# A mixed convolution, pooling and MLP layer on one core: weight splits, a broadcast row and side work given other places in the order

## The chip, the cores and the metric

The kernel runs on one core of one Trainium2 chip. The metric is the device time of one execution in microseconds (us), the median of several runs. In the profile PE is the matrix engine (TensorE), PEld its weight loads, DVE the vector engine, ACT the scalar engine, POOL GpSimd and SP the engine that issues most DMAs. L145 is line 145 of the kernel.

## What is computed

One decoder layer on x of 2048 tokens by 1024 channels, all in float32. Shift, scale and gate of both halves come from a vector c through one large matrix.

```
mod = silu(c) @ w_ada + b_ada                      # sh1, sc1, g1, sh2, sc2, g2
h = x * (1 + sc1) + sh1
z = h @ w_in                                       # 1024 -> 3 * 512 + 512
y_conv = gate_b * short_conv(gate_c * v_conv)      # 3 taps, causal
y_pool = (means over 2, 4, 8, 16 tokens minus token) @ w_pool * pool_scale
x = layer_norm(alpha * x + (1 + g1) * (concat(y_conv, y_pool) @ w_out))
h = x * (1 + sc2) + sh2
f = square(relu(h @ w_mlp_in)) @ w_mlp_out         # 1024 -> 4096 -> 1024
x = layer_norm(alpha * x + (1 + g2) * f)
```

## The kernel before

**Splits and triples.** A float32 matrix is used as the sum of two parts, hi and lo. `split` (L144 to L146) casts the source to hi on ACT (L145) and subtracts hi from the source on DVE (L146). `mm3` (L151) multiplies with three matmuls (L152 to L154): hi by hi, hi by lo, lo by hi. One call of `mm3` is called a triple here; it counts a beat while side work is open.

**Block schemes.** Large products are not done as eight block products but by schemes with fewer products of sums of blocks (seven for two by two blocks; 26 in the last stage). So there is much vector work on sums of blocks: of weights before a product, of results behind it.

**Stages.** The tokens are in two blocks of 1024. For each block: `in_proj_0` or `in_proj_1` (the input projection, four groups; in the second block `in_proj_1`, seven products of eight triples for each group), `out_proj` (seven products, 112 triples) and `first_map` (the MLP's first matrix, "MLP-up": eight groups `up` of seven products of eight triples). `first_map` ends in sums of result blocks (`sums`, L1107), stored to DRAM in `usum` by POOL (`stored`, L1105). Some sums are written in place over cells that have been stored before, so DVE waits there until the store has read them. At the end of block 0 the sums of the last group are kept as `owed` and are done within `in_proj_1` (`flush`). After both blocks `down` does the second matrix in 26 products (`PRODUCTS`) of four steps (gp) each, with operands loaded from `usum` and from the MLP's second weights, raw (`in_w`) or summed (`wsum`).

**The product of seven.** `seven` (L626) makes `product(i, ...)`. It takes the next weight block of the generator `ready` (load into an r tile on SP, and for `block_weights`, L591, four sums on DVE when the third block is taken), splits it into two w tiles, and issues the 24 matmuls. The eviction or sum of the result comes behind it in the caller. There are six w tiles (three pairs) and five r tiles; the 28 h tiles hold the other operands.

**Order.** Instructions are written out in program order; the framework lays them out on each engine's queue by the time at which it reckons them ready, the earlier in the program first among those that are ready. Each queue then runs strictly in order. `issue_after` ties an instruction behind another of its engine; `behind(ins)` (L578) makes everything issued inside it wait for `ins`, on whatever engine.

**Side work.** `sums_down` (L1184) makes the summed weights `wsum` by DMAs from DRAM to DRAM on POOL, 80 of 512 KB: a copy, and later one that adds (L1188). One is issued at each triple whose number is in `W_BEATS`, counted from the start of `in_proj_1`; that stage has the triples 1 to 224, `out_proj` 225 to 336, `first_map` of block 1 those from 337 to 784. `first_map` of block 1 has 48 beats of its own for `second_side`: loads and dot products for the gate g2 (`gate_dot`), and `gate_row` with `row_by_dram` (L223): the 1024 gates are transposed, stored to `grow` and read back into all partitions (`bc`). A job is begun at its beat and finished three beats later.

**Down.** `operand(n, gp)` (L1237) loads and splits four steps ahead. `later = prepared(...)` (L1192) prepares the residual: it loads the rows `ag` and `ab` (L287, scaled in L1194 and L1195), then one tile of `nsave` after another, works on it and stores it to `rsave`; two jobs in each product. `finish` (L1287) reads it, for the first time at product 10.

```
            if n > 0 and gp % 2 == 0:
                next(later, None)
```

The functions that the change touches, and what calls them:

Of the kernel before, what the change touches and what calls it, by code (L numbers as in the profile page):

```python
# [13 lines left out]
P = 128  # L14
# [5 lines left out]
KD = D // P  # L20
# [7 lines left out]
WINDOWS = (2, 4, 8, 16)  # L28
HALO = 16
Q = 256  # L30
W_BEATS = {*range(64, 208, 7), *range(360, 776, 7)}
QUARTERS = slice(0, 256), slice(256, 512)

SLOTS = 26
# [68 lines left out]
G2 = 40  # L103
# [4 lines left out]
def tile_hybrid_layer(ctx: ExitStack, tc: tile.TileContext, opening, xT, x, wada, win,  # L108
                      wins, wpool, wout, wmix, w1, w2, rows, out):
    nc = tc.nc  # L110
# [11 lines left out]
    def mk(p, shape, dt, tag, bufs):  # L122
        names[0] += 1
        return p.tile(shape, dt, name=f"{tag}_{names[0]}", tag=tag, bufs=bufs)
# [4 lines left out]
    def t_o(w=T, dt=F32):  # L129
        return mk(big, [P, w], dt, "o", 10)  # L130
# [7 lines left out]
    def t_ps():  # L138
        return mk(pp, [P, H], F32, "ps", 8)

    def t_tmp():
        return mk(sm, [P, H], F32, "tmp", 1)

    def split(src, hi, lo):  # L144
        high = nc.scalar.copy(hi, src)  # L145
        return high.ins, nc.vector.tensor_tensor(lo, src, hi.bitcast(F32), op=ALU.subtract).ins  # L146


    beside_products, beats = [], [0]

    def mm3(ps, whi, wlo, xhi, xlo, first, last, goes_on=False):  # L151
        nc.tensor.matmul(ps, whi, xhi, start=first, stop=False, skip_group_check=goes_on)  # L152
        nc.tensor.matmul(ps, whi, xlo, start=False, stop=False, skip_group_check=goes_on)  # L153
        done = nc.tensor.matmul(ps, wlo, xhi, start=False, stop=last, skip_group_check=goes_on)  # L154
        if beside_products:
            beats[0] += 1
            if beats[0] in W_BEATS:
                with behind(done.ins):
                    next(beside_products[0], None)
# [42 lines left out]
    mod = cp.tile([P, 48], F32, name="mod")  # L202
# [17 lines left out]
            nc.scalar.copy(dst[:, hs], banks[h])  # L220


    def row_by_dram(dst, cols, n):  # L223
        ps, r = t_ps(), t_tmp()
        nc.tensor.transpose(ps[:KD, :P], cols, ident)
        nc.scalar.copy(r[:KD, :P], ps[:KD, :P])
        nc.gpsimd.dma_start(grow[n].rearrange("(k p) -> k p", k=KD), r[:KD, :P])  # L227
        nc.gpsimd.dma_start(dst, grow[n].partition_broadcast(P))

    cond_banks = spread(silu)  # L230
    keep_warm(ident, ident, WARM[1])
# [22 lines left out]
    grow = tc.dram_tile([2, D], F32, name="grow")  # L254
# [17 lines left out]
    def dot(f, r):  # L272
        return nc.vector.scalar_tensor_tensor(r, r, 1.0, cond, op0=ALU.mult, op1=ALU.mult,
                                              accum_out=acc[:, f : f + 1])
# [71 lines left out]
    def parts(src, t=t_h):  # L346
        hi, lo = t(), t()
        split(src, hi, lo)
        return hi, lo
# [227 lines left out]
    @contextmanager  # L577
    def behind(ins):  # L578
        traced = nc.cur_bb.bb.instructions
        n = len(traced)  # L580
        yield
        for i in traced[n:]:
            if i.engine != nc.tensor.engine:
                tc.add_manual_dep(i, ins.name, mybir.DependencyInfo(
                    mybir.DependencyClass.NoSync if i.engine == ins.engine else mybir.DependencyClass.Sync,
                    mybir.DependencyReason.DATA), reason="behind")
# [39 lines left out]
    def seven(ready, B, first_w=None):  # L626
        made = [first_w] if first_w else []

        def product(i, banks, new):
            hi, lo = made.pop() if made else parts(next(ready), t_w)  # L630
            for p in range(2):
                if new:
                    banks[p] = t_ps()
                for k in range(4):
                    bh, bl = B[ORDER[i][1], k // 2]
                    ks = slice((k % 2) * H, (k % 2) * H + H)
                    cs = slice(p * H + k * P, p * H + k * P + P)
                    mm3(banks[p], hi[:, cs], lo[:, cs], bh[:, ks], bl[:, ks], new and k == 0, k == 3,
                        not new)

        return product

# [549 lines left out]
    def prepared(order, raw, g2):  # L1192
        ag, ab = row(t_o(D), rows[0]), row(t_o(D), rows[1])
        nc.scalar.mul(ag, ag, ALPHA)  # L1194
        nc.scalar.mul(ab, ab, ALPHA)  # L1195

        def gated_weights(r):
            for hs in halves:
                tt(r[:, hs], r[:, hs], g2[:, halves[0]], ALU.mult)

        def residual(r):
            tt(r, r, ag, ALU.mult)
            tt(r, r, ab, ALU.add)

        jobs = [(nsave[t], rsave[t], residual) for t in order]
        jobs += [(w2[w, gp], wsum[W_KEPT - 8 + i, gp], gated_weights) for i, w in enumerate(raw) for gp in range(4)]
        loaded, worked = [], []
        for job in jobs + [None, None]:
            if worked:
                nc.sync.dma_start(*worked.pop())  # L1210
            if loaded:
                (_, dst, work), r = loaded.pop()
                work(r)
                worked.append((dst, r))
            if job:
                r = t_r()
                nc.sync.dma_start(r, job[0])
                loaded.append((job, r))
            yield

    def down(g2, close):
# [15 lines left out]
        def operand(n, gp):  # L1237
            s, ws, sign = PRODUCTS[n][:3]
            if n >= last - 1:
                ws = ((W_KEPT + n - last + 1, 1),)  # L1240
            r = t_r()
            nc.sync.dma_start(r, usum[s, gp].rearrange("p b g n -> p (b g n)"))
            qs = [t_w(F32) for _ in ws]
            for q, (w, _) in zip(qs, ws):
                nc.sync.dma_start(q, w2[w, gp] if w < 8 else wsum[w - 8, gp])
            q = qs[0]
            for more, (_, plus) in zip(qs[1:], ws[1:]):
                tt(q, q, more, ALU.add if plus > 0 else ALU.subtract)
            hi, lo = t_h(), t_h()
            if sign > 0:  # L1250
                split(r, hi, lo)
            else:
                nc.scalar.mul(hi, r, -1.0)
                nc.vector.scalar_tensor_tensor(lo, r, -1.0, hi.bitcast(F32), op0=ALU.mult, op1=ALU.subtract)
            return hi, lo, *parts(q)

        def unit(ps, i, ops, first, end, goes_on, cs=slice(0, H)):
            uh, ul, wh, wl = ops
            for p in range(2):
                us = slice((i // 2) * H + p * Q + (i % 2) * P, (i // 2) * H + p * Q + (i % 2) * P + P)  # L1260
                ws_ = slice(p * H + cs.start, p * H + cs.stop)
                mm3(ps, uh[:, us], ul[:, us], wh[:, ws_], wl[:, ws_], first and p == 0, end and p == 1, goes_on)
# [40 lines left out]
        def last_product(ops):  # L1303
            for i, R in enumerate(rows_of(LATE)):
                for cs in [lo_] if i < 3 else QUARTERS:
                    ps = banks[(last - 1) % 2][i][:, cs]
                    for gp in range(4):
# [9 lines left out]
        ready = [operand(*x) for x in stream[:4]]  # L1317
        later = prepared(sorted(range(16), key=lambda R: (min(final[R % 8 // 2, d] for d in range(2)), R)),
                         [PRODUCTS[n][1][0][0] for n in (last - 1, last)], g2)
        for k, (n, gp) in enumerate(stream):  # L1320
            if n == last:
                break
            if k + 4 < len(stream):
                ready.append(operand(*stream[k + 4]))
            ops = ready.pop(0)
            _, _, _, new, reads = PRODUCTS[n]
            if gp == 0 and new:
                banks[n % 2] = [t_ps() for _ in range(4)]
            if n > 0 and gp % 2 == 0:
                next(later, None)  # L1330
            for i in range(4):
                unit(banks[n % 2][i], i, ops, new and gp == 0, gp == 3, not new)
            if gp == 3:
                for t, d, c in reads:
                    read(t, d, c, banks[n % 2])
                    if final[t, d] == n:
                        finish(t, d)
# [88 lines left out]
    def gate_dot(f):  # L1426
        r = t_o(D)
        nc.sync.dma_start(r, wada[f - G1])
        yield
        dot(f, r)  # L1430

    def gate_row():
        biased(G2, G2 + KD)
        g2 = mk(sm, [P, D], F32, "bc", 1)
        yield
        row_by_dram(g2, mod[:, G2 : G2 + KD], 1)
        gate.append(g2)

    def timed(jobs):
        due = {}  # L1440
        for beat in range(48):
            for _ in due.pop(beat, ()):
                pass
            if beat in jobs:
                next(jobs[beat])
                due[beat + 3] = jobs[beat]
            yield
# [3 lines left out]
        return timed(dict(zip((5, 11, 13, 18, 20, 26), sums)))  # L1451

    def second_side():
        rows_ = [gate_dot(f) for f in range(G2, G2 + KD)] + [gate_row()]
        return timed(dict(zip((4, 6, 11, 13, 18, 20, 25, 27, 33), rows_)))

    gate = []

# [25 lines left out]
    ready = []  # L1484
# [64 lines left out]
```

## Time and profile before

| | |
|---|---|
| median of 3 runs | 1732.97 us (1732.69 to 1733.95) |
| profiled execution | 1726.58 us, span 1724.7 us |
| granted clock of TensorE, mean | 0.994 |
| PE busy | 1692.8 us (98%) |
| DVE busy | 1402.6 us (81%) |
| ACT busy | 844.1 us (49%) |
| POOL busy | 377.9 us (22%) |
| moved by DMA | 469.45 MB, 272 GB/s |

Busy time is the share of the span in which an engine works on an instruction; waits are listed by the engine that waited, with the line that released it. The stages in the profile's time: block 0 to about 580 us, `in_proj_1` to 740, `out_proj` of block 1 to about 820, its `first_map` to about 1140, then `down`.

### The profile page before, as it was taken

To read this page: it belongs to the slowest core of one execution; us is meant where nothing else is said; L and a number is where in the kernel's file an instruction comes from. 1 tells how busy PE (TensorE), PEld (TensorE's weight loads), DVE (VectorE), ACT (ScalarE), POOL (GpSimd) and SP (SyncE) were. 2 spreads that over 40 slices of the span, in tenths; PEclk is the share of its full clock that TensorE was granted. 3 is DMA by queue.
4 is the path that set the end of the run, shared out by engine and by line. 5 is a ranking of instruction groups with operands and counts; after the bars stand their busy time and mean duration, and the time that the engine had idled before them with its cause. 6 is when DMAs were issued, how large, how long until landed. Compare 5 with 4: busy or idle time off the path is not lost. (4 is left out here: it accounts for less than half of the span.)

```text
span 1724.7 us, 22033 instructions
## 1 busy us (share of the span) xinstructions
PE 1692.8 (98%) x7519; PEld 1399.9 (81%) x7519; DVE 1402.6 (81%) x2138; ACT 844.1 (49%) x1160; POOL 377.9 (22%) x687
## 2 busy tenths in 40 slices
PE   9999999999999899999999999889999999999998
PEld 8888888888888688888887888768888888888886
DVE  8997798898886766896887777658888777897898
ACT  6323358556555733446754445346543434434554
POOL 0222221344543202201154555430000000000000
PEclk9999999999999999999999999999999999999999
DMA  9998876567764847975899999899999989786782
GB/s 386 349 334 321 305 261 254 194 202 247 235 219 145 269 147 209 262 253 209 259 265 278 274 271 275 239 333 363 346 342 339 351 321 359 273 324 225 259 293 98
DMA packets 149216, 469.45 MB, mean 272 GB/s; under 512 B 20456, under 2 KB 20976, under 8 KB 149104
## 3 DMA queue, kind: packets, MB, share of 16 engines
q1 hardware_dynamic: 93184, 303.38, 48.9%
q0 software_dynamic: 55920, 164.67, 31.2%
q8 instruction: 58, 0.95, 0.2%
q14 instruction: 54, 0.44, 0.1%
HBM read 350.01 MB, written 159.91 MB: 296 GB/s over the span
## 5 line engine op out<-in xcount | busy, mean ns | idle before, releaser
L154 PE MATMUL ps<-h,w 128*128 128x512 f32 x1312 | 512.9, 392 | 13.0 <-DVE w L146 12.9
L152 PE MATMUL ps<-h,w 128*128 128x512 f32 x1312 | 512.4, 391 | 1.0 <-ACT w L145 0.9
L153 PE MATMUL ps<-h,w 128*128 128x512 f32 x1312 | 512.7, 391 | 0.0
L153 PE MATMUL ps<-h,h 128*128 128x512 f32 (+1 forms) x1064 | 413.7, 389 | 8.4 <-DVE h L146 8.4
L152 PE MATMUL ps<-h,h 128*128 128x512 f32 (+1 forms) x1064 | 413.1, 388 | 0.9 <-DVE h L162 0.9
L154 PE MATMUL ps<-h,h 128*128 128x512 f32 (+1 forms) x1064 | 413.4, 389 | 0.0
L154 PEld LDWEIGHTS ps<-h,w 128*128 128x128 f32 x1312 | 247.6, 189 | 66.6 <-DVE w L146 15.6
L152 PEld LDWEIGHTS ps<-h,w 128*128 128x128 f32 x1312 | 247.2, 189 | 54.0 <-ACT w L145 2.3
L153 PEld LDWEIGHTS ps<-h,w 128*128 128x128 f32 x1312 | 247.2, 188 | 51.7
L1105 POOL DMA_DIRECT2D usum<-o x416 | 226.0, 555 | 271.9 <-DVE o L162 147.5
L145 ACT CAST w<-r 128x1024 fp32r<-128x1024 f32 x156 | 164.1, 1053 | 208.1 <-PE ps L153 187.1
L146 DVE TENSOR_TENSOR w<-r,w 128x1024 fp32r<-128x1024 f32 x156 | 189.9, 1220 | 69.2 <-ACT w L145 68.1
L153 PEld LDWEIGHTS ps<-h,h 128*128 128x128 f32 x1064 | 200.3, 188 | 50.1 <-DVE h L146 9.2
L145 ACT CAST h<-r 128x1024 fp32r<-128x1024 f32 (+1 forms) x136 | 136.2, 1008 | 213.5 <-PE ps L153 89.0
L152 PEld LDWEIGHTS ps<-h,h 128*128 128x128 f32 x1064 | 200.2, 188 | 42.0 <-DVE h L162 1.1
L154 PEld LDWEIGHTS ps<-h,h 128*128 128x128 f32 x1064 | 200.3, 188 | 40.6
L162 DVE TENSOR_TENSOR o<-o,o 128x256 f32<-128x256 f32 (+2 forms) x458 | 201.0, 486 | 20.7 <-DMA usum<-o 18.6
L146 DVE TENSOR_TENSOR h<-r,h 128x1024 fp32r<-128x1024 f32 (+1 forms) x136 | 157.4, 1164 | 65.5 <-ACT h L145 65.1
L145 ACT CAST h<-w 128x1024 fp32r<-128x1024 f32 x104 | 109.1, 1049 | 99.1 <-DVE w L162 90.5
L146 DVE TENSOR_TENSOR h<-w,h 128x1024 fp32r<-128x1024 f32 x104 | 126.7, 1218 | 25.0 <-ACT h L145 24.8
L162 DVE TENSOR_TENSOR o<-o,ps 128x512 f32<-128x512 f32 x184 | 122.4, 681 | 29.2 <-PE ps L154 27.6
L162 DVE TENSOR_TENSOR o<-o 128x256 f32<-128x256 f32 (+1 forms) x176 | 81.8, 468 | 17.6 <-ACT o L1093 8.8
(166 smaller groups left out, 1426.4 us busy)
## 6 DMA issues: line engine op xcount, KB each, us to landing
usum<-o POOLq DMA_DIRECT2D x416, 128.0 KB, 5.3
r<-usum SPq DMA_DIRECT2D x104, 512.0 KB, 5.5
w<-wsum SPq DMA_DIRECT2D x76, 512.0 KB, 7.2
w<-in_w SPq DMA_DIRECT2D x72, 512.0 KB, 6.6
r<-in_w SPq DMA_DIRECT2D x68, 512.0 KB, 6.3
wsum<-in_w POOLq DMA_DIRECT2D x56, 512.0 KB, 9.1
wsum<-wsum POOLq DMA_DIRECT2D x24, 512.0 KB, 7.5
msum<-o POOLq DMA_DIRECT2D x18, 512.0 KB, 6.9
```

The source lines that it names most:

```text
L145: high = nc.scalar.copy(hi, src)
L146: return high.ins, nc.vector.tensor_tensor(lo, src, hi.bitcast(F32), op=ALU.subtract).ins
L152: nc.tensor.matmul(ps, whi, xhi, start=first, stop=False, skip_group_check=goes_on)
L153: nc.tensor.matmul(ps, whi, xlo, start=False, stop=False, skip_group_check=goes_on)
L154: done = nc.tensor.matmul(ps, wlo, xhi, start=False, stop=last, skip_group_check=goes_on)
L162: return nc.vector.tensor_tensor(out_, a, b_, op=op)
L1105: nc.gpsimd.dma_start(usum[slot, g // 2, :, b, g % 2, :], z)
```

## The change

Four places are changed. (1) In `seven`, behind the 24 matmuls of a product, the next weight block is taken and split at once and kept in `made` for the next call. The first product of a group still splits its own. (2) `W_BEATS` has 26 numbers, six apart, where it had 21, seven apart, in the input projection; the numbers from 360 on stay, so the list of 80 jobs is used up earlier. (3) `row_by_dram` becomes `to_dram`, which stores the gate row only; the broadcast is a job of its own, `gate_back`, issued four beats later. (4) `later` starts with product 2 of `down`, not 1, and its two steps there are tied behind the newest matmul (`newest`).

```
-W_BEATS = {*range(64, 208, 7), *range(360, 776, 7)}
+W_BEATS = {*range(56, 210, 6), *range(360, 776, 7)}
...
-    beside_products, beats = [], [0]
+    beside_products, beats, newest = [], [0], []
...
         done = nc.tensor.matmul(ps, wlo, xhi, start=False, stop=last, skip_group_check=goes_on)
+        newest[:] = [done.ins]
...
-    def row_by_dram(dst, cols, n):
+    def to_dram(cols, n):
         ps, r = t_ps(), t_tmp()
         nc.tensor.transpose(ps[:KD, :P], cols, ident)
         nc.scalar.copy(r[:KD, :P], ps[:KD, :P])
         nc.gpsimd.dma_start(grow[n].rearrange("(k p) -> k p", k=KD), r[:KD, :P])
-        nc.gpsimd.dma_start(dst, grow[n].partition_broadcast(P))
...
                     mm3(banks[p], hi[:, cs], lo[:, cs], bh[:, ks], bl[:, ks], new and k == 0, k == 3,
                         not new)
+            for r in ready:
+                made.append(parts(r, t_w))
+                break
...
-            if n > 0 and gp % 2 == 0:
-                next(later, None)
+            if n > 1 and gp % 2 == 0:
+                with behind(newest[0]) if n == 2 else nullcontext():
+                    next(later, None)
...
     def gate_row():
         biased(G2, G2 + KD)
         g2 = mk(sm, [P, D], F32, "bc", 1)
+        gate.append(g2)
         yield
-        row_by_dram(g2, mod[:, G2 : G2 + KD], 1)
-        gate.append(g2)
+        to_dram(mod[:, G2 : G2 + KD], 1)
+
+    def gate_back():
+        yield
+        nc.gpsimd.dma_start(gate[0], grow[1].partition_broadcast(P))
...
-        rows_ = [gate_dot(f) for f in range(G2, G2 + KD)] + [gate_row()]
-        return timed(dict(zip((4, 6, 11, 13, 18, 20, 25, 27, 33), rows_)))
+        rows_ = [gate_dot(f) for f in range(G2, G2 + KD)] + [gate_row(), gate_back()]
+        return timed(dict(zip((4, 6, 11, 13, 18, 20, 25, 27, 33, 37), rows_)))
```

## The prediction

> **What bounds the kernel now.** I read the page first, then the waits of TensorE, then the busy time by stretches, and last the timelines around each place where TensorE stood still.
>
> ```profile
> span 1724.7 us, 22033 instructions
> ...
> PE 1692.8 (98%) x7519; PEld 1399.9 (81%) x7519; DVE 1402.6 (81%) x2138; ACT 844.1 (49%) x1160; POOL 377.9 (22%) x687
> ```
>
> TensorE (PE) is busy 98% of the span, so nothing can be won but its idle time (31.9 us, of which about 8 lie at the start and behind the last matmul) and what a lowered clock adds.
>
> ```profile
> PE ps L154 <- DVE w L146: 12.9, 5, 5.4
> PE ps L153 <- DVE h L146: 8.4, 1, 8.4
> ...
> PE ps L152 <- ACT w L145: 0.9, 2, 0.7
> ```
>
> In the waits of TensorE (total us, times, longest) nearly all of it is the second half of a split: the subtraction of line 146 on VectorE (DVE), for weights (w) five times, for an operand of the last stage (h) once. The timeline of PE says where:
>
> ```profile
> 574.51 0.50 PE L152 MATMUL ps<-h,w 128*128 128x512 f32 x1 [0.69 <-ACT w L145]
> ...
> 597.01 0.80 PE L154 MATMUL ps<-h,w 128*128 128x512 f32 x1 [5.39 <-DVE w L146]
> ...
> 914.77 0.50 PE L154 MATMUL ps<-h,w 128*128 128x512 f32 x1 [2.13 <-DVE w L146]
> ...
> 1110.98 0.50 PE L154 MATMUL ps<-h,w 128*128 128x512 f32 x1 [4.59 <-DVE w L146]
> ...
> 1159.47 0.80 PE L153 MATMUL ps<-h,h 128*128 128x512 f32 x1 [8.41 <-DVE h L146]
> ```
>
> I call the stalls A (574), B (597, in the second block's input projection), C (1110, group 7 of its MLP-up) and D (1159, the start of the down stage). Each costs more than its gap, as matmuls counted in stretches show (us; PE busy and count; PEld, DVE, ACT, POOL likewise; clock; DMA share; GB/s):
>
> ```profile
> 585.00:625.00 40.00, 34.61 (x141) 28.08 (x140) 32.01 (x47) 21.23 (x27) 7.60 (x15) 0.91 0.64 211
> 625.00:665.00 40.00, 40.00 (x179) 33.12 (x178) 26.80 (x30) 13.39 (x17) 7.89 (x11) 1.00 0.63 179
> ...
> 705.00:745.00 40.00, 40.00 (x179) 33.12 (x178) 32.46 (x35) 18.21 (x22) 6.00 (x9) 1.00 0.93 307
> ...
> 903.00:946.00 43.00, 40.83 (x180) 33.17 (x179) 34.23 (x62) 20.31 (x25) 20.40 (x36) 1.00 1.02 281
> ...
> 1032.00:1075.00 43.00, 43.00 (x192) 35.50 (x191) 34.56 (x63) 21.77 (x27) 23.92 (x42) 1.00 1.00 281
> ...
> 1097.00:1118.00 21.00, 16.41 (x66) 13.06 (x65) 11.74 (x28) 6.83 (x10) 11.81 (x23) 0.92 0.92 241
> 1118.00:1140.00 22.00, 22.00 (x98) 17.95 (x97) 11.55 (x18) 10.92 (x14) 10.25 (x16) 1.00 1.06 317
> 1140.00:1161.00 21.00, 12.59 (x52) 10.01 (x53) 14.40 (x31) 8.40 (x10) 6.46 (x12) 0.88 1.05 346
> 1161.00:1204.00 43.00, 43.00 (x188) 35.52 (x187) 37.81 (x34) 27.70 (x32) 3.23 (x6) 0.98 0.98 358
> 1204.00:1290.00 86.00, 86.00 (x381) 71.28 (x380) 72.55 (x69) 39.32 (x48) 0.00 (x0) 1.00 0.93 344
> ```
>
> An undisturbed stretch holds 192 matmuls in 43 us, 0.224 us each. B: 179 - 141 = 38 missing, 8.5 us. C: 21 us should hold 93.8, 66 are there, 27.8 missing, 6.2 us. D: 93.8 - 52 = 41.8 before 1161 and 4 behind it, 10.3 us. The stretch 903 to 946 lacks 12, 2.7 us. The excess over the gaps is the clock: 0.91, 0.92 and 0.88 in B, C and D. The Trainium skill ("TensorE: Matmul & The Clock Gate", What's actually happening) has the array at half rate after an idle window of about 3.4 us, until a busy one has passed. The trace agrees: the gap of 2.13 us left the clock at 1.00, those of 4.59 us and more did not. Its window would give 1.7 us for each, 5.1 in all, where the counts give 3.1, 1.6 and 1.9, 6.6; I keep the counts.
>
> **The change, part by part.**
>
> *Splits moved up.* Inside the products of one group, the next product's load, split and (at the third block) sums get a place in program order behind the current matmuls and ahead of their evictions, sums and stores. The count of instructions is the same: 1.05 us of cast on ScalarE (ACT) and 1.22 us of subtraction each. Stall B shows who stood in front:
>
> ```profile
> 585.97 1.05 ACT L145 CAST w<-r 128x1024 fp32r<-128x1024 f32 x1 [0.51 <-DMA r<-winsum]
> ...
> 597.70 1.05 ACT L145 CAST w<-r 128x1024 fp32r<-128x1024 f32 x1 [4.51 <-DMA r<-winsum]
> ...
> 590.19 1.08 DVE L162 TENSOR_TENSOR o<-o,o 128x256 f32<-128x256 f32 x3
> ...
> 595.75 1.21 DVE L146 TENSOR_TENSOR w<-r,w 128x1024 fp32r<-128x1024 f32 x1
> ```
>
> The cast of product 2's weights was done at 587.0, its subtraction began at 595.75; DVE worked all that time on the sums still owed by the block before (o<-o,o) and on the splits of later inputs, which product 2 doesn't need. With the split ahead of them it ends by about 590, before PE needs it (591.2), so the gap and its clock loss go. What is late next is product 3: its cast waited for its load until 597.70, its subtraction would end 1.05 + 1.22 later at 600.0, while PE would reach it at 591.2 + 24 x 0.224 = 596.6. Its load too now stands ahead of the inputs' loads on SyncE's (SP) queue, so the 3.4 us are an upper bound; I keep 1.5 of them. B gains 8.5 - 1.5 = 7.0 (bounds 5.1 and 8.5). A is a cast late behind the activations of the same product's join, which it now precedes: 0.7. The inputs' splits, now one place later, are wanted a product or more later.
>
> *Gate row in two steps.* The store and the broadcast that waited for it stood back to back on GpSimd's (POOL) queue:
>
> ```profile
> 1093.59 0.55 POOL L228 DMA_DIRECT2D bc<-grow  x1 [5.65 <-DMA grow<-tmp]
> ...
> 1096.14 11.81 DMA wsum<-wsum
> ...
> 1108.36 0.76 DVE L162 TENSOR_TENSOR o<-o,o 128x256 f32<-128x256 f32 x2 [5.81 <-DMA usum<-o]
> ```
>
> (The second row is from the chain of waits.) POOL stood 5.65 us; then the broadcast and three sums of weights went out together, and the stores of the block sums (usum) behind them landed at 1108. DVE waited 5.81 us for them, because it writes the stored cells again, and C's subtraction stood behind that wait. Four beats later the row has long landed, so the broadcast waits for nothing but its beat; behind it on POOL are stores and sums. At two other group ends, with no gate row, the same place costs PE 2.13 us (row above) or less. So C shrinks to something like 0 to 2.1; I take 1.3 left and 4.9 gained, bounds 4.1 and 6.2. If the cover of four beats were too short, the 5.65 us would stand again.
>
> *Beats.* 26 beats instead of 21 lie in the input projection, so the 80 sums of weights end at matmul triple 731, not 766. The block's MLP-up ends at 784, so the last 53 triples (53 x 3 x 0.224 = 36 us) are free of them, where five stood. That is the stretch in front of D:
>
> ```profile
> 1131.11 1.81 POOL L1188 DMA_DIRECT2D wsum<-in_w  x2 [0.75 <-DMA usum<-o]
> ...
> 1135.99 18.63 DMA usum<-o
> ...
> 1154.71 0.76 DVE L162 TENSOR_TENSOR o<-o,o 128x256 f32<-128x256 f32 x2 [6.31 <-DMA usum<-o]
> ...
> 1145.27 0.81 SPq L287 DMA_DIRECT2D o<-in_rows  x2
> ...
> 1160.41 1.06 ACT L1194 ACTIVATE o<-o 128x1024 f32<-128x1024 f32 x1 [12.39 <-DMA o<-in_rows]
> ```
>
> A store issued at 1135.99, just behind the last sums of weights, took 18.63 us to land; DVE stood 6.31 us for it and the operand's subtraction stood behind DVE. The DMA share was 1.06 and 1.05 (rows 1118 to 1161). Without five copies of 512 KB (2.5 MB; at the 346 GB/s of that row some 7 us of all the engines, more as they also write it back) the store lands before DVE comes to it. The other end: the loads of the first operands fill the engines by themselves and nothing is won.
>
> *Residual's preparation later.* Its rows and first tile (each 512 KB) were loaded inside the same rush, and the last row quoted shows ACT standing 12.39 us on those rows, with operand casts queued behind. From product 2 on, and in its two steps tied to the matmuls just issued, SP holds its later loads and ACT its later casts behind that wait; operands are loaded four steps ahead, 4 x 24 x 0.224 = 21 us, which covers a wait of 12. If that lead is not there, up to 12 us come back at product 2. With both edits D loses its 10.3 us but for 1.5, for an operand that is late next: 8.8 (bounds 0 and 10.3).
>
> *What is added.* Five more sums in the input projection: share 0.63 to 0.93 there, against 1.00 in the stretch 1032 to 1075. The Trainium skill ("DMA: Bandwidth & Descriptors", Issuing engines are not separate DMA queues) says that all queues end on the same 16 engines, which speaks against gaining by another place on POOL: the bytes cost the same. By that rule alone beats give nothing; the rows with and without room in the engines decide here. The other cost is the weight pool's three pairs:
>
> ```profile
> ACT w L145 <- PE ps L153: 187.1, 76, 9.0
> ...
> 300.07 1.06 ACT L145 CAST w<-r 128x1024 fp32r<-128x1024 f32 x1 [0.61 <-PE ps L153]
> ...
> 306.24 1.22 DVE L146 TENSOR_TENSOR w<-r,w 128x1024 fp32r<-128x1024 f32 x1
> ```
>
> Casts already start when a pair comes free (76 waits for PE). While groups 0 and 1 alternate, group 1's next pair is now held over five products of group 0, which then turn over two pairs, with one product (5.4 us) for a split. Between nothing and 2.0 us for each of ten products (the lag in these rows is 307.4 - 300.1 = 7.4 us) I take 1.4 us for everything added, because the split now also precedes the operand work that made that lag.
>
> **Sum.** 0.7 + 7.0 + 4.9 + 8.8 - 1.4 = 20.0 us. The profiled execution took 1726.58 us (span 1724.7 and 1.9 around it), so 1706.6 there; the median of the runs is 1732.97, 6.4 above it, which I carry over: 1713.0. With all four stalls gone (0.7 + 8.5 + 6.2 + 10.3 = 25.7) and the 2.7 us at 914 too, 28.4, it would be 1704.6, and nothing added costs less than nothing; with the poor ends (5.1 + 4.1 + 5, less 3) some 11, 1722.
>
> **The rivals.** (1) D only moves: loads fill the DMA engines, or ACT and SP stand on the rows at product 2. For it: share 0.98 and 0.93 up to 1290, with PE coming 10 us sooner. Against: 2.5 MB and the rows' rush are gone. 20.0 - 8.8 = 11.2: 1721.8. Chance 0.14. (2) The splits don't move, as they already start when a pair is free, and what holds DVE is work placed before them anyway: A and B stay, 12.3, so 1720.7. For it the 76 waits, against it the 8.7 us between cast and subtraction in B. Chance 0.10. (3) Slower: the two pairs. It decides from a lag of 7.4 us on, where 10 x (7.4 - 5.4) = 20 eats the gain; in the trace one reached 9.5:
>
> ```profile
> 875.79 1.06 ACT L145 CAST w<-r 128x1024 fp32r<-128x1024 f32 x1
> ...
> 884.13 2.35 DVE L146 TENSOR_TENSOR w<-r,w 128x1024 fp32r<-128x1024 f32 x2
> ```
>
> At a mean lag of 8.1 it costs 27 us: 7 slower, 1740. Against it: no stall stands in those ten products now. Chance 0.14. Small losses in new places that leave it at 1733: 0.05.
>
> **The numbers.** The forecast has 0.57. 0.2% is 3.5 us, about what a measurement of this kernel can tell from no change. Faster: 0.57 + 0.14 + 0.10 = 0.81; same 0.05; slower 0.14. The range 1703 to 1727 holds the forecast with its bounds and the first two rivals (with some 5 us for both together), 0.81 in all.
>
> **What would show it.** Right: no wait of PE for L146 near 597; clock 1.00 there; no wait of POOL for the row's store; no sum of weights in the last 36 us of MLP-up, and usum stores there landing in less than 10 us; PE without a gap of 8 us at the start of the down stage. Wrong: new waits of PE for w near 285 to 325 and 835 to 880 (the two pairs), casts waiting for the rows at product 2 with PE behind them, or the wait of 5 us at 597 in its old size.

## The result and the profile after

The changed kernel takes 1711.05 us in the median of 4 runs (1709.55 to 1713.73), the kernel before 1732.83 (1730.49 to 1733.95): 0.9878 of it, interval 0.9861 to 0.9895. In a second set it took 0.9865 (0.9848 to 0.9882). Forecast were 1713 us, range 1703 to 1727. The profiled execution went from 1726.58 to 1709.94 us.

The page and the waits of TensorE (total us, times, longest) of the changed kernel:

```profile
span 1708.1 us, 22023 instructions
...
PE 1689.0 (99%) x7519; PEld 1397.1 (82%) x7519; DVE 1399.6 (82%) x2138; ACT 844.0 (49%) x1160; POOL 378.0 (22%) x687
```

```profile
PE ps L154 <- DVE w L146: 3.6, 4, 1.3
PE ps L152 <- ACT o L733: 2.1, 1, 2.1
PE ps L153 <- DVE h L146: 1.6, 1, 1.6
PE ps L152 <- ACT w L145: 1.4, 1, 1.4
```

The engines do the same work. What went is waiting: 12.9 us for weights became 3.6, 8.4 us for the first operands of the down stage became 1.6. A wait of 2.1 us for an eviction (L733) is new. The stretches answer to those of before:

```profile
585.00:625.00 40.00, 38.81 (x171) 31.80 (x171) 36.17 (x55) 25.91 (x34) 9.18 (x17) 1.00 0.71 232
...
705.00:745.00 40.00, 39.48 (x175) 32.36 (x173) 28.81 (x33) 16.43 (x20) 7.25 (x10) 1.00 0.99 296
903.00:946.00 43.00, 43.00 (x191) 35.43 (x190) 34.01 (x64) 20.71 (x26) 20.75 (x35) 1.00 1.02 263
...
1097.00:1118.00 21.00, 20.16 (x89) 16.37 (x89) 13.21 (x26) 9.37 (x13) 12.89 (x23) 1.00 1.04 266
1118.00:1140.00 22.00, 22.00 (x99) 18.23 (x98) 14.59 (x30) 12.43 (x14) 7.45 (x15) 1.00 0.97 331
1140.00:1161.00 21.00, 19.36 (x86) 15.72 (x85) 17.70 (x22) 7.93 (x8) 4.56 (x9) 1.00 1.03 347
1161.00:1204.00 43.00, 43.00 (x192) 35.60 (x191) 32.08 (x28) 28.06 (x37) 0.00 (x0) 1.00 0.90 346
```

At B 171 matmuls stand where 141 stood, at C 89 for 66, at D 86 and 192 for 52 and 188, and the clock is at 1.00 in all of them. Of these stretches only 705 to 745 lost: 175 for 179.

The rows that show the three causes gone, from the timelines of the changed kernel: the split of product 2 at B, what is late next there (product 3), DVE's wait for the stores in front of C, and the operand at D.

```profile
590.65 1.22 DVE L146 TENSOR_TENSOR w<-r,w 128x1024 fp32r<-128x1024 f32 x1
...
599.54 0.50 PE L154 MATMUL ps<-h,w 128*128 128x512 f32 x1 [1.19 <-DVE w L146]
...
1099.51 0.76 DVE L163 TENSOR_TENSOR o<-o,o 128x256 f32<-128x256 f32 x2 [0.82 <-DMA usum<-o]
...
1144.42 0.50 PE L153 MATMUL ps<-h,h 128*128 128x512 f32 x1 [1.64 <-DVE h L146]
```

The time in which the usum stores issued between 1097 and 1150 us landed, first before, then after:

```profile
DMA to landing us min/median/max: 3.2/10.4/19.2
```

```profile
DMA to landing us min/median/max: 4.6/7.1/11.3
```

Two of the signs named in the prediction did not come out to the letter. The longest of these stores took 11.3 us, not less than 10. And the last 36 us of MLP-up, which ends at 1131 here, are not free of sums of weights: the last one goes out some 18 us before the end, since POOL comes to it later than its beat. In the kernel before the last ones went out at 1131 to 1133, some 7 us before the end.

```profile
1113.05 0.94 POOL L1191 DMA_DIRECT2D wsum<-in_w  x1 [0.83 <-DMA usum<-o]
```

### The profile page after: what moved, and what is told of

It reads as the page before. It is cut to its first block, busy times and chain, and to the rows that moved or that the text cites. A ratio compares the mean times of both kernels' runs of the same rounds, so it can differ in the third digit from the quotient of the medians.

```text
span 1708.1 us, 22023 instructions
## 1 busy us (share of the span) xinstructions
PE 1689.0 (99%) x7519; PEld 1397.1 (82%) x7519; DVE 1399.6 (82%) x2138; ACT 844.0 (49%) x1160; POOL 378.0 (22%) x687
## 4 chain that ended last, share of the span: by engine, by line
PE 81%; DMA 7%; DVE 5%; issue 4%; ACT 1%; POOL 1%; SPq 0%; DVEq 0%; POOLq 0%; ACTq 0%
PE ps L152 26%; PE ps L154 26%; PE ps L153 26%; DMA usum<-o 4%; DVE o L163 3%; PE ps L487 3%; PE ps L862 1%; DVE w L146 1%; DMA msum<-o 1%; DMA w<-in_w 1%; DMA r<-in_xT 1%; DMA r<-in_w 0%; POOL wsum L1191 0%; DMA r<-wosum 0%; DVE r L163 0%
## 5 line engine op out<-in xcount | busy, mean ns | idle before, releaser
L163 DVE TENSOR_TENSOR o<-o,o 128x256 f32<-128x256 f32 (+2 forms) x458 | 200.5, 487 | 11.1 <-DMA usum<-o 7.9
L163 DVE TENSOR_TENSOR o<-o,ps 128x512 f32<-128x512 f32 x184 | 122.5, 682 | 22.8 <-PE ps L154 20.9
L163 DVE TENSOR_TENSOR o<-o 128x256 f32<-128x256 f32 (+1 forms) x176 | 82.1, 469 | 17.5 <-ACT o L1096 8.0
```

Source lines behind the costliest of these rows:

```text
L163: return nc.vector.tensor_tensor(out_, a, b_, op=op)
```

## The experiments

All edits are counted against the kernel before, run on the same chip in the same set; the changed kernel stands at 0.9865 to 0.9878. It ran in other sets than the kernels that leave one edit out, so a difference to it is one of such ratios. The order of instructions on each engine in the traces makes the runs easy to read. Beats and gate row move only places on POOL; splits move rows on ACT, DVE and SP, none on POOL; the later preparation moves rows on ACT, DVE and SP. TensorE's order depends on the splits alone: with them some matmuls within a few products change places, and leaving out one of the other three edits changes nothing in it.

### Each edit taken out of the changed kernel

Without the splits:

```
-            for r in ready:
-                made.append(parts(r, t_w))
-                break
```

> The changed kernel without the splits behind the matmuls; the other three edits stay. Theory 1 (each edit has its own stall, as predicted): the stall at 597 us is back with its 5.4 us and about 3 us of clock, so 7 us over the changed kernel's 1711.05, 1718; starts of the down stage and of group 7 stay undisturbed. Rival (splits already started when a pair came free, so this edit moves nothing): within 2 us of 1711, and no gap over 2 us near 597.

Measured 0.9933 (0.9918 to 0.9948): some 10 us worse than the changed kernel. The timeline of PE has B back; C and D are not back:

```profile
599.25 0.79 PE L154 MATMUL ps<-h,w 128*128 128x512 f32 x1 [6.55 <-DVE w L146]
```

The rival is out: this edit alone moves the subtraction. The loss is larger than 7, as gaps of 1.9, 1.6 and 2.1 us stand at 734, 874 and 921 us; the third stood in the kernel before too, the first two are new. At 734 and 921 a weight is late on DVE, at 874 a sum of results (L163) for which PE waits. Gaps at the same two new places come with the beats alone (1.1 and 1.7 us), and in no kernel that has the splits or the old beats: they are a cost of the new beats that the splits cover.

Without the new beats:

```
-W_BEATS = {*range(56, 210, 6), *range(360, 776, 7)}
+W_BEATS = {*range(64, 208, 7), *range(360, 776, 7)}
```

> The changed kernel with the old beats (21 sums of weights in the input projection, the last five 5 products later). Theory 1: sums of weights are again beside the last 36 us of the second MLP-up, a usum store there takes over 10 us to land, and PE stands 3 to 8 us at the start of the down stage: 1715 to 1720. Rival (the residual's rows alone made that stall): within 2 us of 1711.

Measured 0.9921 (0.9906 to 0.9936), some 8 us worse. The chain of waits, then DVE and PE:

```profile
1122.50 18.22 DMA usum<-o
```

```profile
1140.81 0.76 DVE L163 TENSOR_TENSOR o<-o,o 128x256 f32<-128x256 f32 x2 [5.90 <-DMA usum<-o]
...
1145.58 0.80 PE L153 MATMUL ps<-h,h 128*128 128x512 f32 x1 [8.01 <-DVE h L146]
```

A store takes 18 us again, DVE stands for it, and D is back at 8.0 us, at the upper end of what was expected, though the residual's rows are not there. The rows did not make D in this form.

Without the second step of the gate row:

```
         to_dram(mod[:, G2 : G2 + KD], 1)
+        nc.gpsimd.dma_start(gate[0], grow[1].partition_broadcast(P))
```

(and `gate_back` not issued)

> The changed kernel with store and broadcast of the gate row back to back. Theory 1: POOL stands 5 to 6 us for the store, the sums behind it bunch, DVE waits about 5 us for usum stores at the end of group 6 and PE stands 3 to 5 us in group 7: 1715 to 1717. Rival (the landing of the stores, not the row, sets that wait): within 2 us of 1711, with POOL standing 5 us all the same.

Measured 0.9893 (0.9876 to 0.9909), 3 to 5 us worse by the middle values; the intervals overlap, so here the trace carries the verdict. POOL, DVE and PE:

```profile
1086.65 0.55 POOL L1442 DMA_DIRECT2D bc<-grow  x1 [4.47 <-DMA grow<-tmp]
...
1087.76 1.89 POOL L1191 DMA_DIRECT2D wsum<-in_w  x2
...
1100.36 0.76 DVE L163 TENSOR_TENSOR o<-o,o 128x256 f32<-128x256 f32 x2 [6.47 <-DMA usum<-o]
...
1102.98 0.79 PE L154 MATMUL ps<-h,w 128*128 128x512 f32 x1 [3.12 <-DVE w L146]
```

The whole sequence of C is back: the wait for the row's store, the sums bunched behind it, DVE standing 6.5 us for the stores behind them, the weights late.

Without the later preparation:

```
-            if n > 1 and gp % 2 == 0:
-                with behind(newest[0]) if n == 2 else nullcontext():
-                    next(later, None)
+            if n > 0 and gp % 2 == 0:
+                next(later, None)
```

> The changed kernel with the residual's preparation from product 1 on and untied. Theory 1: rows and first tile are loaded in the rush before the down stage, ACT stands about 10 us on the rows, and PE stands 2 to 5 us there: 1713 to 1716. Rival A (the beats alone cured that stall): within 2 us of 1711. Rival B (the rows alone made it): 8 us and more, 1719.

Measured 0.9921 (0.9901 to 0.9942; one of four runs is 5 us above the others), 7 to 10 us worse by the middle values and more than the 2 to 5 expected. ACT and PE:

```profile
1141.42 1.06 ACT L1197 ACTIVATE o<-o 128x1024 f32<-128x1024 f32 x1 [9.33 <-DMA o<-in_rows]
...
1146.20 0.56 PE L152 MATMUL ps<-h,h 128*128 128x512 f32 x1 [3.52 <-ACT h L145]
```

ACT stands 9.3 us for the rows, the casts behind it are late, and PE waits for one of them: another releaser than in D, ACT instead of DVE. With the lowered clock behind it and two gaps of 0.7 and 0.8 us beside it, the start of the down stage costs 6 to 7 us more than in the two traces of the changed kernel, counted by the start times of the same matmuls.

### Each edit alone

> The kernel before with the splits behind the matmuls alone. Theory 1 (each edit has its own stall): the 5.4 us at 597 and the clock behind it go, but for 1.5; the 4.6 us in group 7 and the 8.4 us before the down stage stay; the new wait of 2 us at 744 appears, if it belongs to this edit: 3 to 7 us less than the kernel before, 0.996 to 0.998. Rival (the edits only help together, because DVE stays behind from one stage to the next): no gain, 1.000.

Measured 0.9941 (0.9928 to 0.9954), 10 us less and so more than the 3 to 7 expected. B is down to 0.2 us; the gap of 2.1 us at 914 is 1.2 and the one in group 7 is 3.1. D stays, at 8.9. There is no gap at 744. So the edits don't need one another, and the splits help at group ends too.

> The kernel before with the new beats alone. Theory 1 (each edit clears the work that stood in front of one stall): the stall of 8.4 us before the down stage falls to 3 to 5 us, because the residual's rows stay beside it; 597 and group 7 stay as before: 4 to 8 us less than the kernel before, 0.9955 to 0.998. Rival (nothing is won there without the later preparation): 0.999 to 1.000.

Measured 0.9970 (0.9959 to 0.9980), 5 us less. ACT and PE at the start of the down stage:

```profile
1154.73 1.06 ACT L1194 ACTIVATE o<-o 128x1024 f32<-128x1024 f32 x1 [10.34 <-DMA o<-in_rows]
...
1159.42 0.79 PE L152 MATMUL ps<-h,h 128*128 128x512 f32 x1 [4.32 <-ACT h L145]
```

D has halved and changed its releaser. It had two layers: DVE behind the stores, and under it ACT behind the rows. B stays (6.6), and the two gaps of 1.1 and 1.7 us named above come in. The stall in group 7 was expected to stay and did not: POOL stands for the row's store as before and DVE for the stores behind it, but PE waits for no weight there, only 1.4 us for an eviction at 1122.

```profile
1093.14 0.56 POOL L1438 DMA_DIRECT2D bc<-grow  x1 [5.04 <-DMA grow<-tmp]
...
1106.71 0.76 DVE L163 TENSOR_TENSOR o<-o,o 128x256 f32<-128x256 f32 x2 [4.31 <-DMA usum<-o]
```

So that sequence does not always reach PE; in the four other kernels that keep it the gap is 3.1 to 4.6 us.

> The kernel before with the gate row in two steps alone. Theory 1: the stall of 4.6 us in group 7 falls to 0 to 2, the others stay: 3 to 6 us less, 0.9965 to 0.998. Rival (the sums of weights still bunch there, or the time comes back as a longer wait before the down stage): 0.999 to 1.000.

Measured 0.9978 (0.9967 to 0.9989), 3.8 us less. No gap over 0.4 us is left in group 7; B (5.5) and D (7.4) stay.

> The kernel before with the residual's preparation later and tied, alone. Theory 1 (the stores behind the late sums make the stall before the down stage, the rows come second): the stall of 8.4 us stays at 6 us or more, 0 to 3 us less, 0.998 to 1.000. Rival (the rows made most of it): 5 us and more less, 0.997 and below.

Measured 0.9997 (0.9988 to 1.0007): nothing. D stays at 7.2 us, with DVE as its releaser, as the first theory has it: the upper layer hides the lower one.

The four alone sum to 0.59 + 0.30 + 0.22 + 0.03 = 1.14%; together they give 1.22 to 1.35%. Each has an interval of about 0.1% to either side, so a plain sum is not excluded, but the traces show two places where the edits depend on each other: the preparation is worth nothing alone and 6 to 7 us once the beats have moved, and the beats bring gaps that the splits cover. So the four losses on leaving one out, 1.56 to 2.08% by the middle values, add up to more than the whole: D comes back, in whole or in part, when either of two edits is left out.

### The new wait at 744 us

In the changed kernel ACT and PE show, where the input projection of block 1 ends:

```profile
740.48 0.58 ACT L733 COPY o<-ps 128x512 f32<-128x512 f32 x1
744.73 1.33 ACT L398 ACTIVATE o<-o,vecs 128x512 f32<-128x512 f32 x2 [3.68 <-DVE o L163]
745.97 0.56 ACT L733 COPY o<-ps 128x512 f32<-128x512 f32 x1
...
746.59 0.50 PE L152 MATMUL ps<-h,h 128*128 128x512 f32 x1 [2.11 <-ACT o L733]
```

The second eviction of the last product stands behind two steps of the convolution, the first of which waits for DVE, and the out projection needs the bank. The splits set this order on ACT; in the kernel before one of the two steps came first and the other behind the eviction. With the old beats the order on ACT is the same, row for row, but the steps come earlier and PE doesn't wait:

```profile
736.64 0.58 ACT L733 COPY o<-ps 128x512 f32<-128x512 f32 x1
741.32 1.34 ACT L398 ACTIVATE o<-o,vecs 128x512 f32<-128x512 f32 x2 [4.09 <-DVE o L163]
742.56 0.57 ACT L733 COPY o<-ps 128x512 f32<-128x512 f32 x1
```

Its size takes both. With the new beats and without the splits PE waits 0.6 to 0.7 us there for this eviction (at 754 and 755 us), with the splits and without the beats not at all. The beats come with DMA engines nearly full (share 0.99 in the stretch above; 0.93 before), which may be why operands and so DVE come later. That the fuller engines make DVE late is only argued; it was not tried apart. Tying the convolution behind the eviction:

```
-                nc.scalar.copy(dst[p], banks[p])
+                kept[:] = [nc.scalar.copy(dst[p], banks[p]).ins]
...
-                conv(j, u[:, hs.start : hs.stop + 2], y[:, hs], w)
+                with tc.issue_after(kept[0]):
+                    conv(j, u[:, hs.start : hs.stop + 2], y[:, hs], w)
```

> The changed kernel with the convolution of the last group tied behind both evictions on ACT. Theory (the wait at 744 us is the second eviction standing behind a convolution step that waits for DVE): the gap of 2.1 us there goes and nothing else moves, 2 to 4 us less than the changed kernel. Rival (the out projection's operands would be late there anyway): the gap stays, with another cause.

> The changed kernel itself once more, beside the other kernels of this set on one chip: 0.988 of the kernel before, with the gaps of its first profile (574, 598, 744, 1026, 1143 us) within 1 us each.

Measured 0.9852 (0.9837 to 0.9868), median 1703.13 us, beside 1705.26 for the changed kernel itself: 2.1 us less, and each of its four runs (1700.97 to 1704.88) lies below each of the changed kernel's (1705.12 to 1708.55), though the intervals of the ratios overlap. In its trace the two evictions go out together and the gap at 744 is gone; one of 1.1 us, for DVE, stands at 756. The repeat had 0.9865 and its gaps within 1.2 us of the first profile's, the largest difference at 598 (none, for 1.2), where 1 us was expected.

```profile
735.86 1.06 ACT L733 COPY o<-ps 128x512 f32<-128x512 f32 x2
739.62 0.73 ACT L398 ACTIVATE o<-o,vecs 128x512 f32<-128x512 f32 x1 [2.69 <-DVE o L163]
```

With the preparation of block 1's inputs moved behind the fifth product as well:

```
-            if g == NC - 1:
-                turn()
             product(5, Z, False)
+            if g == NC - 1:
+                turn()
```

> The same, and the next block's inputs prepared behind the fifth product of the last group instead of before it. Theory (the wait at 574 us is the cast of the last product's weights standing behind these preparations on ACT): that gap of 1.4 us goes too, 3 to 6 us less than the changed kernel. Rival (the preparations are then late themselves): a new gap of 1 us or more between 580 and 610.

Measured 0.9857 (0.9842 to 0.9872): nothing more. A is gone from the timeline, but three gaps stand a little later:

```profile
596.86 0.50 PE L154 MATMUL ps<-h,w 128*128 128x512 f32 x1 [1.18 <-DVE w L146]
...
602.72 0.50 PE L152 MATMUL ps<-h,w 128*128 128x512 f32 x1 [0.80 <-ACT w L145]
...
603.97 0.50 PE L154 MATMUL ps<-h,w 128*128 128x512 f32 x1 [0.53 <-DVE w L146]
```

So the theory (the preparations stand in front of the cast) holds, and by these gaps its rival (they are late themselves) too; but a gap like the first stood in the changed kernel's first profile as well (599), and one profile can't tell it from chance.

### Sums of weights spread further

```
-W_BEATS = {*range(56, 210, 6), *range(360, 776, 7)}
+W_BEATS = {*range(56, 210, 6), *range(230, 336, 14), *range(360, 776, 8)}
```

(on the kernel with the tied eviction)

> The changed kernel with the eviction tied ahead of the convolution, and eight of the sums of weights moved from the MLP-up, where the engines of the DMA are full, into the out projection, where their share is 0.6 to 0.9; one at every eighth triple in the MLP-up. Theory (the left gaps of 0.5 to 1.3 us at group ends are stores landing late behind sums): those gaps go, 1 to 3 us less than the kernel with the tied eviction alone, 0.984 of the kernel before. Rival (those gaps come from DVE's own order): 0.985, no change, or slower by a new wait in the out projection.

Measured 0.9863 (0.9846 to 0.9879), against 0.9852 for the tied eviction alone: no gain. The gaps at group ends did shrink (one of 0.4 us is left of those between 860 and 1140), but 0.8, 0.7 and 1.1 us came up in the out projection, at 756, 784 and 802. The load was moved, not taken away. Of all kernels run, the changed one with the tied eviction has the lowest middle value, with intervals that overlap those of the last two kernels and of the changed one.

## Why the prediction was right, and where it was off

The profiled gain is 16.6 us (forecast 20.0), that of the medians 21.8. By terms of the sum, with 0.224 us for each missing matmul:

- **B**: 179 - 171 = 8 missing, 1.8 us left of 8.5. Gain 6.7, forecast 7.0. What was named as late next, product 3, is what is late, with 1.19 us of gap where 1.5 was kept.
- **C**: 93.8 - 89 = 4.8 missing, 1.1 us, and these belong to a gap of 0.8 us for an eviction at 1115; the stall in group 7 itself is gone. Gain 5.1, forecast 4.9. The mechanism was shown both ways, by the gate row alone and by leaving it out; but that the beats alone take this gap away too was not foreseen.
- **D**: 93.8 - 86 = 7.8 missing, 1.7 us left of 10.3. Gain 8.6, forecast 8.8. The forecast took the two edits together and could not say which does what; the runs put the upper layer on the beats and the lower on the rows. At product 2 ACT does stand for the rows, as was weighed there:

```profile
1186.50 1.06 ACT L1197 ACTIVATE o<-o 128x1024 f32<-128x1024 f32 x1 [6.79 <-DMA o<-in_rows]
```

  but PE waits for nothing after 1144.42 until the tail; the lead of four steps covers it.
- **A**: wrong. A gap of 0.7 us was to go; it is 1.4 in this profile and 0.8 in the repeat. The step that failed is what the cast was said to stand behind. On ACT the same rows stand ahead of it in both kernels: activations of the next block's inputs and the join of the product before (L1092 and L1093, now L1095 and L1096). The join of the same product, which the cast now precedes in the program, came behind it in the kernel before too. First before, then after:

```profile
569.87 1.05 ACT L1092 ACTIVATE o<-o 128x1024 f32<-128x1024 f32 x1
...
571.52 1.05 ACT L1093 ACTIVATE o<-o 128x1024 f32<-128x1024 f32 x1
...
573.41 1.04 ACT L145 CAST w<-r 128x1024 fp32r<-128x1024 f32 x1
```

```profile
571.21 1.04 ACT L1095 ACTIVATE o<-o 128x1024 f32<-128x1024 f32 x1
...
572.86 1.04 ACT L1096 ACTIVATE o<-o 128x1024 f32<-128x1024 f32 x1
...
574.75 1.04 ACT L145 CAST w<-r 128x1024 fp32r<-128x1024 f32 x1
```

- **What is added**: mis-sized. 1.4 us was taken for two pairs and a fuller input projection. The two pairs cost nothing: PE waits for nothing between 240 and 345 and between 800 and 890. The input projection's end costs 4.0 us, 2.1 of gap and the rest of clock (17 matmuls in 6 us, below), by an order on ACT that the forecast had not looked at, and by the beats.
- **Not in the sum**: the stretch 903 to 946 gained 11 matmuls, 2.5 us; gaps of 0.6 and 1.3 us stand at 987 and 1027, where the kernel before had one of 0.5: 1.4 lost. A cost 0.7 more.

6.7 + 5.1 + 8.6 + 2.5 - 4.0 - 1.4 - 0.7 = 16.8, for 16.6 measured. The medians gained 5 us more than the profiled executions, since the one of before lay 6.4 us below its median and the one after 1.1 below; that this difference carries over was an assumption of the forecast and didn't hold. So the three large terms were right in mechanism and size, but that 1713 lies within 2 us of the median is luck: the profiled execution was forecast 3.3 us too low (1706.6 for 1709.94), and the carry was 5.3 us too high. The profiled run of before may have been a good one: in its 24 runs beside the kernels with the beats, the gate row or the preparation alone the fastest took 1724.73 us at a mean clock of 0.995, the slowest 1733.47 at 0.991, and the profiled one had 0.994.

Rival 1 (D only moves) is out by the trace of the down stage, rival 2 (splits don't move) by the splits alone, rival 3 (two pairs) by the empty waits there.

## What to carry to other kernels

When an engine's queue runs strictly in order, look at what stands in front of the late instruction rather than at the instruction: here a split, a broadcast and a row load were each late or harmful only by the neighbour in their queue, and moving them cost no work. A stall can have layers: an edit worth nothing alone may be worth several microseconds once another one has gone, so read the releaser of what is left before judging it. And a new order must be read to its end, because it puts some other instruction behind a wait, as the eviction at 744.

## What the runs showed of the hardware

The forecast took it from one gap of 2.13 us that such a gap leaves the clock alone. That isn't so in every run. First the changed kernel behind its gap of 2.11 us, then the kernel with the gate row alone behind one of 2.13 us at 915, then the kernel before at the same place (stretch, PE busy and count, PEld, DVE, ACT, POOL, clock, DMA share, GB/s):

```profile
746.00:752.00 6.00, 5.41 (x17) 4.27 (x18) 6.00 (x9) 3.07 (x7) 1.60 (x3) 0.72 0.81 260
```

```profile
915.00:921.00 6.00, 5.53 (x17) 4.44 (x18) 5.93 (x10) 2.59 (x3) 4.36 (x8) 0.72 0.97 305
```

```profile
915.00:921.00 6.00, 6.00 (x27) 4.94 (x27) 5.61 (x10) 3.75 (x5) 3.82 (x7) 1.00 1.03 320
```

17 matmuls instead of 27 in 6 us. Some 0.5 us of that is the end of the gap; the other 1.7 us are the clock, as much as behind C and D (1.6 and 1.9). The Trainium skill ("TensorE: Matmul & The Clock Gate", What's actually happening) lets the clock fall after an idle window of about 3.4 us that runs freely; here gaps of 2.1 us were enough in two of these three runs, so the length of the gap alone didn't decide it. The traces show what does. Between 20 and 1690 us the stretches at half clock last 3.41 us or twice or three times that, and within each trace they begin whole multiples of 3.41 us apart. On that grid, here around the gap at 744:

```profile
743.78:747.19 3.41, 1.30 (x7) 0.74 (x6) 3.41 (x5) 1.80 (x3) 1.10 (x2) 1.00 0.56 175
747.19:750.60 3.41, 3.41 (x10) 2.63 (x9) 3.41 (x5) 1.13 (x3) 1.05 (x2) 0.50 0.79 232
```

In all 14 traces a full clock was halved behind every such stretch in which TensorE stood idle for 1.93 us or more (2.11 above), and behind none with 1.85 or less; it takes no stretch that is idle throughout. The gap of 2.13 us in the kernel before lay across two stretches, with 0.9 and 1.2 us in them; that of the kernel with the gate row alone lay in one. So the cost of a stall of about 2 us depends on where it falls, and differs from run to run of the same kernel: of the two gaps of about 2 us in the repeat, the one at 745 lowered the clock and the one at 1143 did not.
